# Earlier loads, fewer low-rank passes and split sums in a hybrid encoder block

## The chip, the cores and the metric

The kernel runs on one core of one Trainium2 chip. The metric is the device time of one launch in microseconds (us), as the median of repeated runs; beside it there is one profiled execution with a trace. The engines are PE (TensorE, matrix products), DVE (VectorE), ACT (ScalarE), POOL (GpSimd, hardly used here) and SP (SyncE, which issues all DMAs of this kernel).

## The reference

One layer of an encoder block on x of 1024 tokens by 1024 features in float32: a gated linear attention (GLA) branch and a windowed attention branch from one input projection, then a SwiGLU feed-forward.

```python
h = _rms_norm(x, norm_mix_g[l])
proj = h @ w_in[l]
(g_q, g_k, g_v, g_r, g_lr_f, g_lr_b,
 s_q, s_k, s_v, gate_a, gate_b) = jnp.split(proj, split_at, axis=-1)
y_gla = _gla_branch(...) @ w_o_gla[l]      # log gate: log_sigmoid(lr @ up + bias) / 16, lr has rank 16 each way
y_swa = _swa_branch(...) @ w_o_swa[l]      # banded attention in blocks of 128, 8 heads on 2 key heads
merged = jax.nn.sigmoid(gate_a) * y_gla + jax.nn.sigmoid(gate_b) * y_swa
x = x + merged @ w_out[l]
h2 = _rms_norm(x, norm_ffn_g[l])
gu = h2 @ w_ffn_in[l]
x = x + (jax.nn.silu(gu[..., :D_FF]) * gu[..., D_FF:]) @ w_ffn_out[l]   # D_FF = 2816
```

The low-rank codes `g_lr_f` and `g_lr_b` are 16 columns each, 32 in all.

## The kernel before

Everything is kept transposed: features on the 128 partitions, tokens along the free dimension in two halves of 512 (`s` = 0, 1). A product in float32 is made of three matmuls in fp32r (`mm3`): each operand is split into a high part (an fp32r copy made on ACT) and a low part (the rest, subtracted on DVE), and high x high, high x low and low x high are summed in PSUM. `wunit` loads a weight unit (`wr`) and splits it so (`wh`, `wl`). Most big products run in a scheme with fewer block products and more additions (lines L300 to L302 for the first stage).

The order of PE's instructions is written out by hand (`tc.manual_schedule` for PE); the other engines' orders are set by a scheduler that knows the dependences. All tiles come from pools; a tag with one buffer is used again only when its last user has finished, and a pool that is opened later can lie on the memory of one that has been closed, with waits on that memory's last users.

The places that the change touches, in order of time:

- **The low-rank codes** (`lr_mm`). The weights are 32 columns repeated three times, 96 wide, in two units of four k-tiles. For each of 8 k-tiles and 2 halves there are three matmuls into a 96-row PSUM tile. The 96 rows go to DRAM (`keep_raw`), and later come back as `lrf`, are multiplied with the norm's factor `rstd` and split into `lrS` (high, low and high again in its three groups of 32 rows), beside the gate's up-projection (`upr`, split to `upS`). The gate matmul is `ch<-lrS,upS`. `upr` and `lrf` live in the pool `ip`.
- **Sums over partitions.** A matmul of ones with the summed squares (`acc`) adds over the partitions and broadcasts the sum; `rsqrt` makes `rstd` of it (Ln and Exp on ACT, then a Newton step of four instructions on DVE, L101 to L104). In the first stage it is called for both halves one after the other, with the buffers "rsl" and "rst" of pool `w0`; `out_stats` does the same late in the kernel.
- **Attention** runs in slots (`todo`); each slot's stages are laid between dense matmuls of another projection (`fill`). `k_prep` and `a_prep` load a block of keys and values (`kvr`, one buffer) or of queries (`qr`, two) from DRAM and normalise it at once. `st` (L186) is the copy of dense results out of PSUM on ACT.
- **The second feed-forward product** (`fo_product`) follows the last call of `ffn_in`. For each step `k` it loads and splits an input (`hload`: `hr`, `hh`, `hl`) and a weight (`a`, split to `wh`, `wl`) and issues 12 matmuls (L1169).

Of the kernel before, what the change touches and what calls it, by code (L numbers as in the profile page):

```python
# [8 lines left out]
F32 = mybir.dt.float32  # L9
# [5 lines left out]
P = 128  # L15
# [15 lines left out]
def body(tc, i, out):  # L31
    nc = tc.nc
    with ExitStack() as root:
# [49 lines left out]
        nc.scalar.preload_act_table_set("natural_log_exp_and_others")  # L83

        g1 = load_const(cst, "g1", i["g1"], (P, KT))
        ones = cst.tile([P, P], F32, tag="ones", name="ones")
        nc.vector.memset(ones, 1.0)
        epst = cst.tile([P, 1], F32, tag="eps", name="eps")
        nc.vector.memset(epst, EPS)
        eps128 = cst.tile([P, 1], F32, tag="eps128", name="eps128")  # L90
# [123 lines left out]
                done = t  # L214


        def lr_mm(b, u):
            h, l = wunit(i["w_lr"][u], 384)
            for kk in range(4):
                k = u * 4 + kk  # L220
                c = slice(kk * 96, (kk + 1) * 96)
                for s in range(2):
                    mm3(b[s][:96], h[:, c], l[:, c], xh[k][s], xl[k][s], k == 0, k == KT - 1)

# [148 lines left out]
        with tc.manual_schedule(engines={mybir.EngineType.PE}):  # L373
            xr[0, 0] = x_load(0, 0)

            wu = chtile((P, 512))
            for _ in range(12):
                mm(wu[:, :P], ones, ones, True, True)
            bq = [[mmtile(), mmtile()] for _ in range(2)]
            us = [wunit(i["w_f"][m, 0]) for m in range(2)]  # L380
            xr[0, 1] = x_load(0, 1)
            for k in range(KT):
                if k < KT - 1:
                    for s in range(2):
# [12 lines left out]
            for u in range(2):  # L397
                lr_mm(bl, u)
            for m in range(2):
                for s in range(2):  # L400
                    keep_raw(("q0", "k0")[m], s, bq[m][s])
            for s in range(2):
                keep_raw("lr", s, bl[s], 96)
            for k in range(KT):
                for s in range(2):
                    x_square(k, s)
            for f in range(0, NG, 2):
                x_first(f)
                if f == 0:
                    for s in range(2):  # L410
                        v = chtile((P, HT))
                        mm(v, ones, acc[s], True, True)
                        rsqrt(rstd[:, s * HT:(s + 1) * HT], v, 1.0 / T, EPS, epst, w0, (P, HT), "", ("rsl", "rst"))
                    vt = chtile((P, KT, 2))
                    for t in range(KT):
                        mm(vt[:, t], acc[t // 4][:, (t % 4) * P:(t % 4 + 1) * P], ones[:, 0:2], True, True)
                    rsqrt(rstdt, vt[:, :, 0], 1.0 / T, EPS, epst, pad, (P, KT), "rt")
                for k in range(2):
                    xcombos(f % 4 + k, f // 4)
            for f in range(NG):  # L420
                x_two(f)
                if f == NG - 1:
                    for k in range(4):
                        r = x_load(k, 1, True)
                        xh[k][1] = xp.tile([P, HT], FR, tag=f"xh{k}1", name=nm("xh"))
                        xl[k][1] = xp.tile([P, HT], FR, tag=f"xl{k}1", name=nm("xl"))
                        x_split(xh[k][1], xl[k][1], r, g1[:, k:k + 1])
                if f:
                    x_last(f - 1)
                x_four(f)  # L430
            x_last(NG - 1)
# [18 lines left out]
        lrf = ip.tile([96, T], F32, tag="lrf", name="lrf")  # L450
        for s in range(2):
            c = slice(s * HT, (s + 1) * HT)
            nc.sync.dma_start(out=lrf[:, c], in_=scr["lr", s][:96])
            nc.vector.tensor_tensor(lrf[:, c], lrf[:, c], rstd[:96, c], op=ALU.mult)
        nc.scalar.activation(lrS[0:96], lrf, AF.Copy)
        nc.vector.tensor_tensor(lrS[32:64], lrf[32:64], lrS[32:64].bitcast(F32), op=ALU.subtract)
# [266 lines left out]

        keys, att = {}, {}

        def k_prep(t):
            kv = sw.tile([P, 4, P], F32, tag="kvr", name=nm("kvr"), bufs=1)
            need(("skv", t))
            nc.sync.dma_start(out=kv.rearrange("p a b -> p (a b)"), in_=scr["skv", t])
            v2 = kv[:, 2:4].rearrange("p a b -> p (a b)")  # L730
            nc.scalar.activation(vSh[t], v2, AF.Copy)
            nc.vector.tensor_tensor(vSl[t], v2, vSh[t].bitcast(F32), op=ALU.subtract)
            keys[t] = norm_rope(kv[:, 0:2], 2, t, kg, 1.0 / 128, EPS, epst)
# [8 lines left out]

        def a_prep(g, n):
            a = att[g, n] = Chunk()
            need((f"sq{g}", n))
            qr = sw.tile([P, 4, P], F32, tag="qr", name=nm("qr"))
            nc.sync.dma_start(out=qr.rearrange("p a b -> p (a b)"), in_=scr[f"sq{g}", n])
# [105 lines left out]
        for n in range(2 * KT):  # L853
# [9 lines left out]
        order = (a_probs, k_prep, a_prep, a_scores, a_turn, k_turn, a_out)  # L863
# [213 lines left out]
        def ffn_in(f, between):  # L1077
# [27 lines left out]
            product(X, wsplit(F.r22, 512), YX["T4"], 4, False, True)  # L1105
            c21, g0 = ctile("c21"), F.g0
            nc.vector.tensor_tensor(c21, X, p1, op=ALU.add)
            nc.vector.tensor_tensor(c21, c21, g0, op=ALU.mult)
            nc.vector.tensor_tensor(c22, c22, u2, op=ALU.mult)
            put("B1" if f < DK else "B2", 1, f % DK, c21)  # L1110
            put("B1" if f < DK else "B2", 2, f % DK, c22)

            if f < DK:
                t1 = hp.tile([P, HT], F32, tag="tx", name=nm("tx"), bufs=4)
# [18 lines left out]
        later = []  # L1133
        steps = [0]

        def hload(key, k, th, tl):
            r = fo1.tile([P, HT], F32, tag="hr", name=nm("hr"), bufs=6)
# [18 lines left out]
        def fo_product(ys, q, key, start, stop, before, after, th=None, tl=None):  # L1156
            for k in range(DK):
                before(k)
                if not (th and tl):
                    steps[0] += 1  # L1160
                pool = fo3 if steps[0] % 3 == 2 else hp
                x = hload(key, k, (th[0], f"a{th[1]}{k}") if th else (pool, "hh"),
                          (tl[0], f"a{tl[1]}{k}") if tl else (pool, "hl"))
                w = wsplit(aq[q, k], 512)
# [27 lines left out]
        with tc.manual_schedule(engines={mybir.EngineType.PE}):  # L1192
# [12 lines left out]
            for k in range(4):  # L1205
# [78 lines left out]
def _layout(n):  # L1284
# [12 lines left out]
    lr = np.tile(w[:, 3072:3104], (1, 3)).reshape(2, 4, P, 96)  # L1297
    d["w_lr"] = np.ascontiguousarray(lr.transpose(0, 2, 1, 3)).reshape(2, P, 384)
# [53 lines left out]
```

## Time and profile before

| | us |
|---|---|
| median of 3 runs | 1671.59 (1671.16 to 1672.97) |
| profiled execution | 1674.78 |
| its span, first to last instruction | 1673.0 |
| PE busy | 1655.1 |
| DVE busy | 1260.0 |
| ACT busy | 892.7 |

The mean granted TensorE clock was 0.998. In a row of the timeline the first number is the start in us, the second the time of the instruction (or of all of a group, with its count as x4), and the bracket at the end tells how long the engine had been idle and what released it. Matmuls overlap, so the time from one start to the next is what one costs. In a row of the waits stand the total, the count and the longest. A row with two times and a colon is a stretch of the span: its length, the busy time of each engine with its count of instructions, the granted clock, the DMA share and GB/s.

### The profile page before, as it was taken

The numbers are of one execution on the slowest core, as the hardware profiler recorded it, in microseconds if no ns is written. First come the engines' busy times: TensorE is split into PE (matmuls) and PEld (weight loads), VectorE is DVE, ScalarE is ACT, GpSimd is POOL, SyncE is SP. The second block draws the span as 40 slices with busy tenths as digits, with TensorE's granted clock in tenths as the row PEclk, the third lists the DMA queues.
The fourth block names the chain that finished last, engine by engine and source line by source line (L and its number), as shares of the span: only waits on it lengthen the run. The fifth ranks groups of instructions, "written<-read, shape, count | busy, mean of one in ns | idle before, by whom it ended". The sixth has DMA issues, their size and how long they took to land.

```text
span 1673.0 us, 23709 instructions
## 1 busy us (share of the span) xinstructions
PE 1655.1 (99%) x7808; PEld 1373.8 (82%) x7808; DVE 1260.0 (75%) x2615; ACT 892.7 (53%) x1881; POOL 0.2 (0%) x4
## 2 busy tenths in 40 slices
PE   9999999999999999999999999999999999999999
PEld 7888888888888788877888888888888888788887
DVE  8756767888874799856886679887778778779755
ACT  8522465687877488776554556433333333354443
POOL 0000000000000000000000000000000000000000
PEclk9999999999999999999999999999999999999999
DMA  7444453344434643227866645353234443496533
GB/s 234 139 137 152 142 158 94 108 139 125 134 114 153 190 133 102 89 76 242 261 215 188 174 141 170 108 170 101 89 110 154 152 145 126 164 333 195 149 97 120
DMA packets 157067, 251.88 MB, mean 151 GB/s; under 512 B 17966, under 2 KB 43438, under 8 KB 156944
## 3 DMA queue, kind: packets, MB, share of 16 engines
q1 hardware_dynamic: 156944, 250.37, 47.9%
q8 instruction: 61, 1.00, 0.3%
q14 instruction: 62, 0.51, 0.1%
HBM read 182.80 MB, written 67.50 MB: 150 GB/s over the span
## 4 chain that ended last, share of the span: by engine, by line
PE 87%; ACT 5%; DVE 4%; DMA 3%; issue 1%; SPq 0%; ACTq 0%; DVEq 0%
PE mm L76 33%; PE mm L300 8%; PE mm L302 7%; PE mm L301 7%; PE ch L76 7%; PE mm L1169 7%; PE ch L1169 5%; PE ch L302 3%; PE ch L300 3%; PE ch L301 3%; PE ch L813 1%; DMA kvr<-skv 1%; ACT p L796 1%; DMA lo<-b 1%; ACT p L802 0%
## 5 line engine op out<-in xcount | busy, mean ns | idle before, releaser
L70 ACT ACTIVATE wh<-wr 128x512 fp32r<-128x512 f32 (+1 forms) x240 | 149.6, 628 | 101.2 <-PE mm L76 75.9
L72 DVE TENSOR_TENSOR wl<-wr,wh 128x512 fp32r<-128x512 f32 (+1 forms) x240 | 164.0, 686 | 45.8 <-ACT wh L70 45.2
L292 ACT ACTIVATE wh<-ws 128x512 fp32r<-128x512 f32 x120 | 76.0, 634 | 178.5 <-PE mm L301 89.1
L76 PE MATMUL mm<-wh,xh 128*128 128x512 f32 x320 | 127.0, 397 | 3.5 <-ACT st L186 3.5
L76 PE MATMUL mm<-wl,xh 128*128 128x512 f32 x320 | 128.2, 401 | 0.0
L76 PE MATMUL mm<-wh,xl 128*128 128x512 f32 x320 | 127.1, 397 | 0.0
L76 PE MATMUL mm<-xh,wh 128*128 128x512 f32 x256 | 103.4, 404 | 0.8 <-ACT wh L70 0.6
L76 PE MATMUL mm<-xl,wh 128*128 128x512 f32 x256 | 101.2, 395 | 0.3 <-DVE xl L245 0.3
L293 DVE TENSOR_TENSOR wl<-ws,wh 128x512 fp32r<-128x512 f32 x120 | 82.4, 687 | 21.6 <-ACT wh L292 21.6
L292 ACT ACTIVATE wh<-wr 128x512 fp32r<-128x512 f32 x60 | 38.0, 634 | 105.3 <-issue 49.5
L292 ACT ACTIVATE wh<-a 128x512 fp32r<-128x512 f32 x66 | 41.9, 635 | 90.3 <-PE ch L1169 42.2
L76 PE MATMUL mm<-xh,wl 128*128 128x512 f32 x256 | 87.7, 405 | 0.0
L293 DVE TENSOR_TENSOR wl<-a,wh 128x512 fp32r<-128x512 f32 x66 | 45.6, 691 | 41.7 <-ACT wh L292 41.3
L76 PEld LDWEIGHTS mm<-wh,xh 128*128 128x128 f32 x320 | 60.6, 189 | 14.4 <-ACT st L186 3.9
L1169 PE MATMUL mm<-hh,wh 128*128 128x512 f32 x176 | 69.1, 392 | 1.4 <-ACT hh L1141 1.4
L1169 PE MATMUL mm<-hl,wh 128*128 128x512 f32 x176 | 69.3, 394 | 0.7 <-DVE hl L1142 0.7
L1169 PE MATMUL mm<-hh,wl 128*128 128x512 f32 x176 | 69.2, 393 | 0.0
L76 PEld LDWEIGHTS mm<-wh,xl 128*128 128x128 f32 x320 | 60.6, 189 | 10.5
L76 PEld LDWEIGHTS mm<-wl,xh 128*128 128x128 f32 x320 | 60.6, 189 | 10.1
L1142 DVE TENSOR_TENSOR hl<-hr,hh 128x512 fp32r<-128x512 f32 x77 | 52.9, 687 | 6.5 <-ACT hh L1141 6.4
L76 PEld LDWEIGHTS mm<-xh,wh 128*128 128x128 f32 x256 | 48.2, 188 | 7.4 <-ACT wh L70 0.8
L76 PEld LDWEIGHTS mm<-xl,wh 128*128 128x128 f32 x256 | 48.2, 188 | 7.3 <-DVE xl L245 0.8
(574 smaller groups left out, 4892.3 us busy)
## 6 DMA issues: line engine op xcount, KB each, us to landing
wr<-in_w_fi_dram SPq DMA_DIRECT2D x102, 256.0 KB, 2.8
wr<-in_w_f_dram SPq DMA_DIRECT2D x80, 256.0 KB, 2.9
wr<-in_w_t_dram SPq DMA_DIRECT2D x80, 256.0 KB, 2.8
B<-c SPq DMA_DIRECT2D x44, 256.0 KB, 2.1
T<-tx SPq DMA_DIRECT2D x44, 256.0 KB, 2.6
a<-in_w_fo_dram SPq DMA_DIRECT2D x44, 256.0 KB, 5.3
hr<-T SPq DMA_DIRECT2D x44, 256.0 KB, 2.7
hr<-B SPq DMA_DIRECT2D x33, 256.0 KB, 4.2
```

The costliest lines, as they stand in the source:

```text
L70: nc.scalar.activation(h, raw, AF.Copy)
L72: nc.vector.tensor_tensor(l, raw, h.bitcast(F32), op=ALU.subtract)
L76: nc.tensor.matmul(o, a, b, start=start, stop=stop)
L292: nc.scalar.activation(h, src, AF.Copy)
L293: nc.vector.tensor_tensor(l, src, h.bitcast(F32), op=ALU.subtract)
L300: nc.tensor.matmul(o, h[:, c], x[kk][0], start=start and kk == 0, stop=False, skip_group_check=True)
L301: nc.tensor.matmul(o, h[:, c], x[kk][1], start=False, stop=False, skip_group_check=True)
L302: nc.tensor.matmul(o, l[:, c], x[kk][0], start=False, stop=kk == nk - 1, skip_group_check=True)
L796: nc.scalar.activation(p[:, h, :w], p[:, h, :w], AF.Exp, bias=nm_[:, h:h + 1], scale=a.rs[:, h:h + 1], accum_out=dn[:, h:h + 1])
L813: nc.tensor.transpose(pt[:, h], a.p[:, h, (kb - a.b0) * P:(kb - a.b0 + 1) * P], ident)
L1142: nc.vector.tensor_tensor(l, r, h.bitcast(F32), op=ALU.subtract)
L1169: nc.tensor.matmul(ys[m], a[:, c], b, start=f0, stop=f1, skip_group_check=True)
```

## The change

Five edits.

1. Low-rank codes: the weight is loaded as 32 columns per k-tile and its high and low part stand side by side in one 64-column operand. Per k-tile and half there is one matmul of the 64 columns with the high part of x and one of the 32 high columns with its low part. The 64 rows in DRAM hold two partial sums, which are added after loading, in three groups of 32 rows, through a new tile `lrb` in `ip` (one buffer).
2. `part_sum`: the sum over partitions takes a split `acc`, two fp32r matmuls in place of one in f32. The parts use the tags of `rsqrt`'s buffers.
3. Attention: the loads are stages of their own (`k_load`, `a_load`), one slot ahead of `k_prep` and `a_prep`, at the end of the slot's stages.
4. The first two steps of the second feed-forward product are loaded at the start of the last `ffn_in`, and their weights split ahead of its last product.
5. In the last `ffn_in` the two gated products (`c21`, `c22`) are put off to later steps.

```diff
-        ones = cst.tile([P, P], F32, tag="ones", name="ones")
+        onesr = cst.tile([P, P], FR, tag="ones", name="ones")
+        ones = onesr.bitcast(F32)
+        def part_sum(v, a, pool):
+            h = pool.tile([P, HT], FR, tag="rsl", name=nm("ah"))
+            l = pool.tile([P, HT], FR, tag="rst", name=nm("al"))
+            nc.scalar.activation(h, a, AF.Copy)
+            nc.vector.tensor_tensor(l, a, h.bitcast(F32), op=ALU.subtract)
+            mm(v, onesr, h, True, False)
+            mm(v, onesr, l, False, True)
...
-                    mm3(b[s][:96], h[:, c], l[:, c], xh[k][s], xl[k][s], k == 0, k == KT - 1)
+                    nc.tensor.matmul(b[s][:64], w[:, k].rearrange("p a b -> p (a b)"), xh[k][s], start=k == 0,
+                                     stop=False, skip_group_check=True)
+                    nc.tensor.matmul(b[s][:32], w[:, k, 0], xl[k][s], start=False, stop=k == KT - 1,
+                                     skip_group_check=True)
...
-                        mm(v, ones, acc[s], True, True)
+                        part_sum(v, acc[s], w0)
...
-            nc.sync.dma_start(out=lrf[:, c], in_=scr["lr", s][:96])
+            lrb = ip.tile([96, HT], F32, tag="lrb", name=nm("lrb"))
+            for g in range(3):
+                nc.sync.dma_start(out=lrf[32 * g:32 * g + 32, c], in_=scr["lr", s][0:32])
+                nc.sync.dma_start(out=lrb[32 * g:32 * g + 32], in_=scr["lr", s][32:64])
+            nc.vector.tensor_tensor(lrf[:, c], lrf[:, c], lrb, op=ALU.add)
...
+        def k_load(t):
+            raws[t] = sw.tile([P, 4, P], F32, tag="kvr", name=nm("kvr"), bufs=1)
+            need(("skv", t))
+            nc.sync.dma_start(out=raws[t].rearrange("p a b -> p (a b)"), in_=scr["skv", t])
+        def a_load(g, n):
+            need((f"sq{g}", n))
+            raws[g, n] = sw.tile([P, 4, P], F32, tag="qr", name=nm("qr"))
+            nc.sync.dma_start(out=raws[g, n].rearrange("p a b -> p (a b)"), in_=scr[f"sq{g}", n])
...
+                if n:
+                    todo[n - 1].append((k_load, n))
+            todo[n].append((a_load, g, t))
+        order = (a_probs, k_prep, a_prep, a_scores, a_turn, k_turn, a_out, k_load, a_load)
+        k_load(0)
...
-            mm(v, ones, acc[:, s * HT:(s + 1) * HT], True, True)
+            part_sum(v, acc[:, s * HT:(s + 1) * HT], fi)
...
+            w = wsplit(F.r22, 512)
+            if f == NFF - 1:
+                for k in range(2):
+                    r, x = early[k]
+                    early[k] = (x, wsplit(r, 512))
+            product(X, w, YX["T4"], 4, False, True)
...
+                    later.append(lambda v=v: gated(*v))
...
+                if th and tl and k < len(early):
+                    x, w = early[k]
...
+                if f == NFF - 1:
+                    for k in range(2):
+                        r = ctile("oc")
+                        nc.sync.dma_start(out=r, in_=i["w_fo"][k, 0])
+                        early.append([r, hload(("B1", 1), k, (hp, "hh"), (hp, "hl"), ctile("oc"))])
```

How the engines' orders change at the places that matter. The names are tiles (output, then inputs), and the brackets the semaphores that the instruction waits for. First PE at the two sums of the first stage, before:

```order
L302 MATMUL mm_478<-xh_101,wl_545 128x512
L76 MATMUL ch_563<-acc_136,ones 128x512
L76 MATMUL ch_573<-acc_137,ones 128x512 [waits PE_49]
L76 MATMUL ch_583<-ones,acc_136 128x2 x4
L76 MATMUL ch_583<-ones,acc_137 128x2 x4
L300 MATMUL mm_622<-xh_87,wh_626 128x512
```

And now:

```order
L76 MATMUL ch_540<-ah_541,ones 128x512
L76 MATMUL ch_540<-al_542,ones 128x512 [waits DVE_49]
L76 MATMUL ch_555<-ah_556,ones 128x512 [waits PE_49,Activation_49]
L76 MATMUL ch_555<-al_557,ones 128x512 [waits DVE_49]
L76 MATMUL ch_570<-ones,acc_136 128x2 [waits PE_49]
```

DVE there, now, from the first step of the first half's rsqrt (`rt_550`) to the subtraction of the second half (`al_557`); the other rows are the combinations of x that later products need:

```order
L111 TENSOR_SCALAR rt_550<-ch_540 128x512 [waits Activation_49]
L278 TENSOR_TENSOR T4l_820<-xr_253,T4h_819 128x512 [waits Activation_49]
L112 TENSOR_TENSOR rt_550<-rt_550,rl_547 128x512 [waits DVE_49,Activation_49]
L278 TENSOR_TENSOR T3l_911<-xr_193,T3h_910 128x512 [waits Activation_49]
L113 SCALAR_TENSOR_TENSOR rt_550<-rt_550,rl_547 128x512 [waits DVE_49]
L297 SCALAR_TENSOR_TENSOR xr_285<-xr_285,g_70,xr_287 128x512
L114 SCALAR_TENSOR_TENSOR rstd<-rt_550,rl_547 128x512 [waits DVE_49]
L295 SCALAR_TENSOR_TENSOR xr_213<-xr_213,ng_134,xr_307 128x512
L278 TENSOR_TENSOR T4l_916<-xr_285,T4h_915 128x512 [waits Activation_49]
L94 TENSOR_TENSOR al_557<-acc_137,ah_556 128x512 [waits Activation_49]
```

The subtraction for the second sum now stands behind the last step of the first half's rsqrt; there was no such instruction before. Next, SP at the end of the first stage, before. `gb` and `ga` are its last stores, `upr` and `lrf` the gate's loads, `wr` weights:

```order
L63 DMA tri<-in_c_tri_dram 128x128 [waits DMAHW4_49,DVE_49]
L445 DMA upr<-in_up_dram 98x1024 [waits DMAHW5_49]
L453 DMA lrf<-lr_427 96x512 [waits DMAHW6_49]
L453 DMA lrf<-lr_431 96x512 [waits DMAHW7_49]
L68 DMA wr_2024<-in_w_t_dram 128x512 [waits DMAHW0_49,DVE_49]
L306 DMA gb_0_1813<-xc_368_1811 128x512 [waits DMAHW1_49,DVE_49]
L68 DMA wr_2042<-in_w_t_dram 128x512 [waits DMAHW2_49,DVE_49]
L306 DMA gb_1_1835<-xc_372_1833 128x512 [waits DMAHW3_49,DVE_49]
L68 DMA wr_2060<-in_w_t_dram 128x512 [waits DMAHW4_49,DVE_49]
L306 DMA ga_1_1856<-xu_353_1769 128x512 [waits DMAHW5_49,DVE_49]
L68 DMA wr_2078<-in_w_t_dram 128x512 [waits DMAHW6_49,DVE_49]
L306 DMA gb_0_1876<-xc_378_1874 128x512 [waits DMAHW7_49,DVE_49]
```

And now:

```order
L322 DMA ga_1_1843<-xu_353_1756 128x512 [waits DMAHW1_49,DVE_49]
L68 DMA wr_2079<-in_w_t_dram 128x512 [waits DMAHW2_49,DVE_49]
L322 DMA gb_0_1863<-xc_378_1861 128x512 [waits DMAHW3_49,DVE_49]
L68 DMA wr_2097<-in_w_t_dram 128x512 [waits DMAHW4_49,DVE_49]
L460 DMA upr<-in_up_dram 98x1024 [waits DMAHW5_49,DMAHW7_49,DMAHW3_49,DMAHW1_49]
L470 DMA lrf<-lr_404 32x512 [waits DMAHW6_49]
L471 DMA lrb_1891<-lr_404 32x512
L470 DMA lrf<-lr_404 32x512 [waits DMAHW0_49]
```

The load of `upr` has moved behind the last store of the stage and waits for four transfers in place of one. Last, ACT in attention's start, before:

```order
L99 ACTIVATE rl_7019<-rl_7019 128x4 [waits Activation_49]
L186 ACTIVATE st_6941<-mm_6697,rstdt 128x512 [waits PE_49]
L186 ACTIVATE st_6977<-mm_6698,rstdt 128x512 [waits PE_49]
L186 ACTIVATE st_6987<-mm_6699,rstdt 128x512 [waits PE_49]
L70 ACTIVATE wh_7044<-wr_7042 128x512 [waits DMAHW3_49,PE_49]
L98 ACTIVATE rl_7132<-ss_7128,eps_76 128x4 [waits DVE_49]
L731 ACTIVATE vSh_6785<-kvr_6946 128x256 [waits DMAHW1_49]
L695 ACTIVATE sq_6950<-kvr_6946 128x256
L186 ACTIVATE st_6997<-mm_6700,rstdt 128x512 [waits PE_49]
```

And now:

```order
L196 ACTIVATE st_6946<-mm_6698,rstdt 128x512 [waits PE_49]
L196 ACTIVATE st_6980<-mm_6699,rstdt 128x512 [waits PE_49]
L196 ACTIVATE st_6990<-mm_6700,rstdt 128x512 [waits PE_49]
L714 ACTIVATE sq_7220<-qr_7182 128x512 [waits DMAHW0_49,DVE_49]
L70 ACTIVATE wh_7050<-wr_7048 128x512 [waits DMAHW4_49,PE_49]
L196 ACTIVATE st_7018<-mm_6701,rstdt 128x512 [waits PE_49]
L760 ACTIVATE vSh_6786<-kvr_6881 128x256 [waits DMAHW2_49]
```

The fourth `st` has moved ahead of `vSh`, and a step on the third block of queries (`sq<-qr`) has moved ahead of that `st`.

More of the change, by code (lines that the diff above doesn't have):

```diff
@@ L214, in slot, with lr_mm @@
                 done = t
[L217 to L221, printed above, removed]
+        def lr_mm(b):
+            raw = wp.tile([P, KT, 32], F32, tag="wr", name=nm("wr"), bufs=4)
+            nc.sync.dma_start(out=raw, in_=i["w_lr"])
+            w = wp.tile([P, KT, 2, 32], FR, tag="wh", name=nm("wh"), bufs=5)
+            nc.scalar.activation(w[:, :, 0], raw, AF.Copy)
+            nc.vector.tensor_tensor(w[:, :, 1], raw, w[:, :, 0].bitcast(F32), op=ALU.subtract)
+            for k in range(KT):
                 for s in range(2):
-                    mm3(b[s][:96], h[:, c], l[:, c], xh[k][s], xl[k][s], k == 0, k == KT - 1)
+                    nc.tensor.matmul(b[s][:64], w[:, k].rearrange("p a b -> p (a b)"), xh[k][s], start=k == 0,
+                                     stop=False, skip_group_check=True)
+                    nc.tensor.matmul(b[s][:32], w[:, k, 0], xl[k][s], start=False, stop=k == KT - 1,
+                                     skip_group_check=True)
         g0s = ExitStack()
@@ L396, in body @@
             bl = [chtile((P, 512)), chtile((P, 512))]
-            for u in range(2):
-                lr_mm(bl, u)
+            lr_mm(bl)
             for m in range(2):
@@ L402, in body @@
             for s in range(2):
-                keep_raw("lr", s, bl[s], 96)
+                keep_raw("lr", s, bl[s], 64)
             for k in range(KT):
@@ L724, in body @@
         keys, att = {}, {}
+        raws = {}
+        def k_load(t):
[6 more added lines that the diff above has]
+            nc.sync.dma_start(out=raws[g, n].rearrange("p a b -> p (a b)"), in_=scr[f"sq{g}", n])
         def k_prep(t):
-            kv = sw.tile([P, 4, P], F32, tag="kvr", name=nm("kvr"), bufs=1)
-            need(("skv", t))
-            nc.sync.dma_start(out=kv.rearrange("p a b -> p (a b)"), in_=scr["skv", t])
+            kv = raws.pop(t)
             v2 = kv[:, 2:4].rearrange("p a b -> p (a b)")
@@ L744, in a_prep @@
             a = att[g, n] = Chunk()
-            need((f"sq{g}", n))
-            qr = sw.tile([P, 4, P], F32, tag="qr", name=nm("qr"))
-            nc.sync.dma_start(out=qr.rearrange("p a b -> p (a b)"), in_=scr[f"sq{g}", n])
+            qr = raws.pop((g, n))
             b = sw.tile([P, 4, P], F32, tag="sq4", name=nm("sq"))
@@ L1104, in ffn_in, with gated @@
             nc.vector.tensor_tensor(u2, u2, r1, op=ALU.mult)
-            product(X, wsplit(F.r22, 512), YX["T4"], 4, False, True)
+            w = wsplit(F.r22, 512)
[4 more added lines that the diff above has]
+            product(X, w, YX["T4"], 4, False, True)
             c21, g0 = ctile("c21"), F.g0
             nc.vector.tensor_tensor(c21, X, p1, op=ALU.add)
[L1108 to L1111, printed above, removed]
+            def gated(j, c, g):
+                nc.vector.tensor_tensor(c, c, g, op=ALU.mult)
+                put("B1" if f < DK else "B2", j, f % DK, c)
+            for v in ((1, c21, g0), (2, c22, u2)):
+                if f < NFF - 1:
+                    gated(*v)
+                else:
+                    later.append(lambda v=v: gated(*v))
             if f < DK:
@@ L1134, in body, with hload @@
         steps = [0]
-        def hload(key, k, th, tl):
-            r = fo1.tile([P, HT], F32, tag="hr", name=nm("hr"), bufs=6)
+        early = []
+        def hload(key, k, th, tl, r=None):
+            if r is None:
+                r = fo1.tile([P, HT], F32, tag="hr", name=nm("hr"), bufs=6)
             nc.sync.dma_start(out=r, in_=scr[(*key, k)])
@@ L1296, in _layout @@
     d["w_t"] = np.ascontiguousarray(np.stack([a.reshape(KT, P, 512) for a in wt]))
-    lr = np.tile(w[:, 3072:3104], (1, 3)).reshape(2, 4, P, 96)
-    d["w_lr"] = np.ascontiguousarray(lr.transpose(0, 2, 1, 3)).reshape(2, P, 384)
+    d["w_lr"] = np.ascontiguousarray(w[:, 3072:3104].reshape(KT, P, 32).transpose(1, 0, 2))
     up = np.zeros((98, 2, 512), f)
```

8 lines of the change are left out of this document (4 added, 4 removed).

## The prediction

> **What bounds the kernel now.** I read the busy shares first, then the chain that ended last.
>
> ```profile
> PE 1655.1 (99%) x7808; PEld 1373.8 (82%) x7808; DVE 1260.0 (75%) x2615; ACT 892.7 (53%) x1881; POOL 0.2 (0%) x4
> PE 87%; ACT 5%; DVE 4%; DMA 3%; issue 1%; SPq 0%; ACTq 0%; DVEq 0%
> ```
>
> PE (TensorE) is busy 1655.1 of 1673.0 us, so it is idle for 18 us in all. Two things shorten such a kernel: fewer PE slots, and the removal of a wait of PE. Any new wait of PE is paid in full, because PE has no slack later in which to make it good. The waits of PE, largest first:
>
> ```profile
> PE mm L76 <- ACT st L186: 3.5, 1, 3.5
> PE mm L1169 <- ACT hh L1141: 1.4, 1, 1.4
> PE mm L1169 <- DVE hl L1142: 0.7, 1, 0.7
> ```
>
> The first is in attention; the other two are the start of the second feed-forward product. Both are places that the change touches.
>
> **Low-rank codes.** 48 matmuls become 32 of the same 512 columns.
>
> ```profile
> 29.46 11.09 PE ch L76 x48
> 197.88 5.44 PE mm L76 x24
> 203.32 0.24 PE ch L76 x2
> ```
>
> On the chain one of the 48 takes 11.09 / 48 = 0.231 us with 96 weight columns, and one of 24 dense ones 5.44 / 24 = 0.227 us with 128. The width of the weights does not set the time, so 64 and 32 columns cost the same slot: 16 fewer are **-3.7 us**, as PE works back to back there.
>
> **Sums over partitions.** Each f32 matmul becomes two on split operands.
>
> ```profile
> 51.28 1.88 PE L76 MATMUL ch<-acc,ones 128*128 128x512 f32 x4
> 52.99 1.84 PE L76 MATMUL ch<-ones,acc 128*128 128x2 f32 x16
> ```
>
> Two sums (four records) take 52.99 - 51.28 = 1.71 us, 0.855 each; two split matmuls take 0.454. Four sums save **-1.6 us**. The two late sums (the output's statistics) have their own free buffers and their accumulators are done us ahead, so I take their copy and subtraction as hidden: 0 to +1 us if they are not.
>
> The second sum of the first stage is another matter. Its high and low parts use the buffers "rsl" and "rst", one each, and the first sum's rsqrt uses the same two until its last step. So the second sum, which follows the first at once on PE, has to wait for the whole rsqrt of the first: Ln, Exp, four steps on DVE, then its own copy and subtraction.
>
> ```profile
> 32.66 0.69 DVE L253 TENSOR_TENSOR acc<-acc,sq 128x512 f32<-128x512 f32 x1 [0.19 <-ACT sq L251]
> 53.34 0.71 DVE L72 TENSOR_TENSOR wl<-wr,wh 128x512 fp32r<-128x512 f32 x1
> 57.17 0.69 DVE L104 SCALAR_TENSOR_TENSOR rstd<-rt,rl 128x512 f32<-128x512 f32 x1
> 53.08 0.68 ACT L98 ACTIVATE rl<-ch,eps 128x512 f32<-128x512 f32 x1
> 54.17 0.62 ACT L99 ACTIVATE rl<-rl 128x512 f32<-128x512 f32 x1
> ```
>
> DVE is a full queue from 32.66 on: 40 places later, two of them tiny, it runs the last step of the first rsqrt at 57.17: (24.5 - 0.3) / 38 = 0.64 us each. In the changed order that step stands 34 places behind the same add: 32.66 + 34 x 0.64 = 54.4, ending at 55.1, less some 0.5 us because one split of the low-rank weights fewer stands ahead: 54.6. The copy on ACT takes some 0.6, like the Exp, and by the place of the subtraction, third behind the last step, DVE ends it near 56.4. PE reaches this point at 51.28 - 3.70 = 47.6, does the first sum until 48.0, and could do both matmuls of the second at once; the last of them cannot start before 56.4. Idle: 56.4 - 48.0 - 0.2 = **+8.2 us**. Bounds: 5.4 if DVE's queue were empty (0.68 + 0.62 + 4 x 0.69 + 0.62 + 0.69), 10 if Ln and Exp get stuck behind neighbours on ACT.
>
> **The gate's loads.** Smaller codes mean more loads and two added sums, but what decides is where the load of the gate's up-projection (upr) stands. Its pool has grown by a tile of 2 KB per partition (lrb) and now reaches into memory whose last users are the final stores of the first stage. In the order of SP the load stood ahead of those stores; now it stands behind the last one and waits for it to land.
>
> ```profile
> 187.08 4.54 DMA upr<-in_up_dram
> 199.21 0.32 SPq L306 DMA_DIRECT2D gb<-xc  x1
> 202.60 0.32 SPq L483 DMA_DIRECT2D qk<-q  x1
> 191.72 1.06 ACT L446 ACTIVATE upS<-upr 98x1024 fp32r<-98x1024 f32 x1 [1.91 <-DMA upr<-in_up_dram]
> 192.15 0.69 DVE L454 TENSOR_TENSOR lrf<-lrf,rstd 96x512 f32<-96x512 f32 x1 [1.16 <-DMA lrf<-lr]
> 192.87 1.22 DVE L447 TENSOR_TENSOR upS<-upr,upS 34x1024 fp32r<-34x1024 f32 x1
> 195.44 1.07 ACT L455 ACTIVATE lrS<-lrf 96x1024 fp32r<-96x1024 f32 x1 [0.26 <-DVE lrf L454]
> 196.64 1.22 DVE L456 TENSOR_TENSOR lrS<-lrf,lrS 32x1024 fp32r<-32x1024 f32 x1
> qk<-q SPq DMA_DIRECT2D x2, 128.0 KB, 2.4
> ```
>
> Before, the codes were ready at 196.64 + 1.22 = 197.9 and the first gate matmul ran at 203.32: 5.4 us to spare. The load of qk waited for the same last store and was issued at 202.60, so upr is issued about then (a time of before; where PE is earlier or later all of this moves along). Then, in series: upr 4.54, copy 1.06, subtraction 1.22, add 0.69, the second half's lrb (one buffer, three issues and a landing like qk's, 0.9 + 2.4), add and multiply 1.38, copy 1.07, subtraction 1.22: 14.5 us, to 217.1. PE gets there at 203.32, so 13.8; the last store can go out some 0.5 us sooner because DVE no longer does the gate's work ahead of it: **+13.3 us**. Bounds: 10.5 if the loads of both halves overlap and land in 2 us, 15 if the twelve small loads queue. PE's order is fixed by hand, so nothing steps in front of the gate matmul; later dense weights are ready by the time it runs.
>
> **Attention.** One wait goes:
>
> ```profile
> 560.50 4.88 DMA kvr<-skv
> 565.41 0.42 ACT L731 ACTIVATE vSh<-kvr 128x256 fp32r<-128x256 f32 x1 [2.04 <-DMA kvr<-skv]
> 566.04 0.67 ACT L186 ACTIVATE st<-mm,rstdt 128x512 f32<-128x512 f32 x1
> 566.76 0.50 PE L76 MATMUL mm<-wh,xh 128*128 128x512 f32 x1 [3.45 <-ACT st L186]
> 567.45 0.63 PE L76 MATMUL mm<-wh,xl 128*128 128x512 f32 x1
> 570.01 0.63 PE L76 MATMUL mm<-wh,xl 128*128 128x512 f32 x1
> 566.80:570.40 3.60, 3.60 (x9) 2.85 (x10) 3.43 (x13) 1.95 (x6) 0.00 (x0) 0.55 0.66 215
> ```
>
> ACT stood at vSh for a load, and the copy out of PSUM (st) that PE needed was behind it. The load still goes to a single buffer and was issued the moment that it was free, so it will hardly land sooner; what helps is that this st now stands ahead of vSh on ACT. A third query load now stands ahead of the st, which I put at 0.7 us of wait left. Then there is the price after the wait: six matmuls from 567.45 to 570.01 are 0.427 us apart instead of 0.227, at a granted clock of 0.55, so about 1.4 us are lost after the wait itself. Gain 3.5 + 1.5 - 0.7 = **-4.3 us** (0 to -5). In the other slots the transposes come some 15 matmuls sooner on PE, 3.4 us; I allow half of that either way.
>
> **Second feed-forward.** Its first two steps' inputs and weights are loaded and split during the last feature.
>
> ```profile
> 1452.65 0.33 SPq L1150 DMA_DIRECT2D a<-in_w_fo_dram  x1
> 1450.00:1455.00 5.00, 5.00 (x24) 4.10 (x22) 2.24 (x4) 0.63 (x1) 0.00 (x0) 1.00 0.27 69
> 1454.95 0.39 PE L302 MATMUL mm<-bt43h,wl 128*128 128x512 f32 x1
> 1456.70 0.49 PE L1169 MATMUL mm<-hh,wh 128*128 128x512 f32 x1 [1.36 <-ACT hh L1141]
> 1457.93 0.72 PE L1169 MATMUL mm<-hl,wh 128*128 128x512 f32 x1 [0.73 <-DVE hl L1142]
> 1459.13 0.63 PE L1169 MATMUL mm<-hh,wh 128*128 128x512 f32 x1
> 1460.83 0.63 PE L1169 MATMUL mm<-hl,wh 128*128 128x512 f32 x1
> 1457.90:1461.20 3.30, 3.27 (x7) 2.36 (x8) 2.81 (x5) 1.95 (x4) 0.00 (x0) 0.52 0.98 356
> ```
>
> From 1454.95 to 1459.13 five slots should take 1.1 us and take 4.2; then some five more are 0.425 apart, at a granted clock of 0.52. That is 3.1 + 1.2 = **-4.3 us**. Two steps are 24 matmuls, 5.4 us of cover, and the third step's load is issued when the first one's was, about 1452.65; by the same steps of loading and splitting it is ready some 1 us ahead of need. Two extra weight loads of 256 KB fall where the DMA share is 0.27. Kept: 0 to -4.4.
>
> **The clock after a wait.** Both long waits above are followed by some 3.5 us at 0.52 to 0.55. The two new ones, 8.2 and 13.3 us, are longer, so I charge each 1.4 us: **+2.8**. The Trainium skill, "TensorE: Matmul & The Clock Gate", section "What's actually happening", says that after an idle window of about 3.4 us the array runs at half clock until it has been busy for about as long; this trace agrees (0.55 over 3.6 us after 3.45 us of idling). By the page each wait would cost 1.7 us, an estimate from it, and the sum would be 0.6 us higher. It speaks against this change.
>
> **Sum.** -3.7 - 1.6 - 4.3 - 4.3 = -13.9; +8.2 + 13.3 + 2.8 = +24.3; together **+10.4 us**. The profiled execution took 1674.8 us (span 1673.0), so 1685.2 by its clock; the median shown is 1671.59, 3.2 lower, and I forecast against that: **1682.0 us**. Within 0.2% (3.3 us) I call it the same.
>
> **The rivals.**
> A. The sum as it stands, 1676 to 1688 by the bounds above: 60%.
> B. The gate matmul is not late: the stores land well before 202.60 (that row shows only when the next load was issued), or the loads that follow are quick. Price 14.7, so -4.3 and 1667.3. It ends on the other side when the loss there, clock included, is below 1.0 us. For it speaks the 5.4 us to spare before; against it, upr and the two splits behind it alone take 6.8 us after the last store was issued at 199.21. 9%.
> C. The second sum does not wait long, because its buffers come free while PE is still behind. Price 9.6: +0.8, 1672.4. Against it speaks the 5.4 us of the shortest chain. 9%.
> D. Neither wait shows: -13.9, 1657.7. 11%.
> E. The new waits come and attention keeps its own, since its load lands no sooner and another evacuation is caught behind it: +14.7, 1686.3, more if the twelve small loads queue. 11%.
>
> A and E are slower; B and D faster; C about the same, with the edges of B and C: slower 0.73, same 0.09, faster 0.18. The range runs from 1666, which leaves out D, to 1689.
>
> **What the profile would show.** The codes: 32 matmuls in 7.4 us. The second sum: PE idle for some 8 us near 48 us with ACT's ah or DVE's al as releaser, then half clock. The gate: upr issued after the last gb store and PE idle for some 13 us before the first matmul of lrS, released by DVE. Attention: no wait near 566 over 1 us. Second feed-forward: 0.23 us from step to step at the start. I am wrong if either of the new waits is missing, or if PE finds a wait there that begins later and ends sooner than the chains above say; the weakest number is the gate's, eight steps in series of which two are small loads never timed in this trace.

## The result

The changed kernel takes 1688.58 us in the median of 5 runs (1686.35 to 1690.55) against 1671.59 us (1670.74 to 1674.23): slower, ratio 1.0099 with a 95% interval of 1.0085 to 1.0114. The forecast was 1682.0. The profiled execution took 1690.42 us with a span of 1688.6, 15.6 more than before.

Busy time and chain of the changed kernel:

```profile
PE 1655.4 (98%) x7792; PEld 1373.5 (81%) x7792; DVE 1263.7 (75%) x2620; ACT 892.0 (53%) x1884; POOL 0.2 (0%) x4
PE 87%; DVE 5%; ACT 3%; DMA 3%; issue 1%; SPq 0%; DVEq 0%; ACTq 0%
```

There are sixteen matmuls fewer, and PE is busy as long as before: some matmuls must have run slower. The span has grown by idle time. The waits of PE (total, count, longest):

```profile
PE ch L76 <- DVE lrS L475: 12.2, 1, 12.2
PE ch L76 <- ACT ah L93: 6.9, 1, 6.9
PE ch L76 <- DVE pl L844: 1.5, 1, 1.5
...
PE ch L76 <- DVE kTl L770: 0.9, 1, 0.9
...
PE mm L76 <- ACT obh L868: 0.6, 1, 0.6
```

The two large waits of before (st at 566, hh and hl at 1456) are gone from the head of the list. Two larger ones stand there: the gate matmul and the second sum.

The second sum in PE's timeline, and the clock behind it (stretch, length, busy times, granted clock, DMA share, GB/s):

```profile
47.13 0.40 PE L76 MATMUL ch<-al,ones 128*128 128x512 f32 x1
54.39 0.80 PE L76 MATMUL ch<-ah,ones 128*128 128x512 f32 x1 [6.87 <-ACT ah L93]
55.54 0.80 PE L76 MATMUL ch<-al,ones 128*128 128x512 f32 x1 [0.35 <-DVE al L94]
56.13 3.41 PE L76 MATMUL ch<-ones,acc 128*128 128x2 f32 x16
54.40:58.00 3.60, 3.25 (x12) 2.65 (x12) 3.04 (x5) 1.23 (x2) 0.00 (x0) 0.50 0.02 5
62.00:63.50 1.50, 1.50 (x5) 1.11 (x5) 1.17 (x4) 0.00 (x0) 0.00 (x0) 0.50 0.00 0
64.00:66.00 2.00, 2.00 (x10) 1.60 (x10) 0.69 (x1) 1.11 (x2) 0.00 (x0) 1.00 0.00 0
```

The second sum's last matmul ran at 55.54, where 56.4 was forecast. But the clock stayed at one half until about 63.8, 9.4 us after the restart, and the sixteen small matmuls (the rows `128x2`) took 3.41 us where they had taken 1.84.

The gate: three rows of SP's timeline, then pieces of the chain that ended last (start, time, what):

```profile
205.05 0.33 SPq L322 DMA_DIRECT2D gb<-xc  x1
207.58 0.40 SPq L460 DMA_DIRECT2D upr<-in_up_dram  x1
215.23 1.24 SPq L471 DMA_DIRECT2D lrb<-lr  x3
205.05 2.46 DMA gb<-xc
212.18 1.06 ACT upS L461
214.52 0.70 DVE lrf L472
216.05 1.92 DMA lrb<-lr
218.14 0.70 DVE lrf L472
218.86 0.70 DVE lrf L473
219.59 1.06 ACT lrS L474
220.67 1.23 DVE lrS L475
221.94 0.79 PE ch L76 x2
```

Here upr is issued 2.5 us after the last store gb, when that has landed, and the gate matmul follows 221.94 - 207.58 = 14.4 us later; the forecast's chain had 14.5.

The start of the second feed-forward product:

```profile
1474.07 0.39 PE L1217 MATMUL mm<-hh,wh 128*128 128x512 f32 x1
1475.89 0.39 PE L1217 MATMUL mm<-hh,wl 128*128 128x512 f32 x1
```

Eight steps in 1.82 us, 0.227 each, with no wait.

Taking the start of the same matmul in both traces gives an account of where the time went:

| stretch (us of before) | measured | forecast |
|---|---|---|
| to 40.4: low-rank codes (0.7 of it in the first 9 us) | -4.4 | -3.7 |
| both sums of the first stage, to 53.0 | +7.5 | +8.2 - 0.8 |
| half clock behind them, to 56.9 | +3.4 | +1.4 |
| wait before the gate matmul, at 203.2 | +12.2 | +13.3 |
| half clock behind it, to 206.4 | +2.8 | +1.4 |
| attention, to 775.8 | -1.5 | -4.3 |
| late sums, to 1063 | -1.2 | -0.8 |
| start of the second feed-forward, to 1460.8 | -4.0 | -4.3 |
| its sixth step, to the end | +0.8 | 0 |
| all (from figures before rounding) | +15.7 | +10.4 |

### The profile page after: what moved, and what is told of

It reads as the page before. It is cut to its first block, busy times and chain, and to the rows that moved or that the text cites. A ratio compares the mean times of both kernels' runs of the same rounds, so it can differ in the third digit from the quotient of the medians.

```text
span 1688.6 us, 23701 instructions
## 1 busy us (share of the span) xinstructions
PE 1655.4 (98%) x7792; PEld 1373.5 (81%) x7792; DVE 1263.7 (75%) x2620; ACT 892.0 (53%) x1884; POOL 0.2 (0%) x4
## 4 chain that ended last, share of the span: by engine, by line
PE 87%; DVE 5%; ACT 3%; DMA 3%; issue 1%; SPq 0%; DVEq 0%; ACTq 0%
PE mm L76 32%; PE mm L316 8%; PE mm L317 8%; PE mm L318 8%; PE mm L1217 7%; PE ch L76 7%; PE ch L1217 5%; PE ch L317 3%; PE ch L318 3%; PE ch L316 3%; PE ch L840 1%; DVE wl L72 0%; DMA gb<-gb 0%; PE ch L647 0%; DMA kvr<-skv 0%
## 5 line engine op out<-in xcount | busy, mean ns | idle before, releaser
L70 ACT ACTIVATE wh<-wr 128x512 fp32r<-128x512 f32 x238 | 148.4, 628 | 111.7 <-PE mm L76 80.2
L72 DVE TENSOR_TENSOR wl<-wr,wh 128x512 fp32r<-128x512 f32 x238 | 162.5, 686 | 54.8 <-ACT wh L70 52.0
L308 ACT ACTIVATE wh<-wr 128x512 fp32r<-128x512 f32 x60 | 37.9, 632 | 104.0 <-issue 48.1
```

The source lines that it names most:

```text
L70: nc.scalar.activation(h, raw, AF.Copy)
L72: nc.vector.tensor_tensor(l, raw, h.bitcast(F32), op=ALU.subtract)
L308: nc.scalar.activation(h, src, AF.Copy)
```

## The experiments

**The gate's loads.** The first run puts the second parts of the codes into lrS, which is free at that time:

```diff
-            lrb = ip.tile([96, HT], F32, tag="lrb", name=nm("lrb"))
+            lrb = lrS[0:96, c].bitcast(F32)
```

> The changed kernel, with the second parts of the low-rank codes loaded into lrS (which is overwritten only later) in place of the new tile lrb, so that the pool ip keeps its old size; the twelve loads and the two additions stay. Theory (the pool's reach moves upr behind the last store): upr is issued near 186 us again, the wait of 12.2 us before the first gate matmul goes and with it 2.8 us of half clock behind it: 15 us faster than the changed kernel, about 1673.5. Rival (the small loads and additions are late in themselves): upr early, but 5 to 10 us of wait remain, 1679 to 1684.

Measured: 1682.54 us, 6.0 faster than the changed kernel; the rival's range. The waits of PE, then rows of SP and DVE of this run:

```profile
PE ch L76 <- DVE lrS L475: 3.9, 1, 3.9
PE mm L76 <- DVE xc L386: 1.9, 1, 1.9
194.30 0.46 SPq L460 DMA_DIRECT2D upr<-in_up_dram  x1
205.29 0.58 SPq L471 DMA_DIRECT2D lrS<-lr  x1
208.75 0.34 SPq L322 DMA_DIRECT2D gb<-xc  x1
209.62 0.42 SPq L471 DMA_DIRECT2D lrS<-lr  x1
206.71 0.69 DVE L472 TENSOR_TENSOR lrf<-lrf,lrS 96x512 f32<-96x512 f32 x1 [3.15 <-DMA lrS<-lr]
208.04 0.68 DVE L386 TENSOR_TENSOR xc<-mm,xp 128x512 f32<-128x512 f32 x1
```

The pool's reach is half of the story: upr is issued ahead of the last four stores again and its 14 us chain is gone. But now the twelve loads alternate with the stores in SP's order. The first addition holds DVE for 3.15 us, xc behind it is late, PE waits for xc, its store gb is late too, and the last loads stand behind that store.

The next run takes the additions and most of the loads away from there: DVE adds the two parts straight from PSUM before they are stored.

```diff
-                keep_raw("lr", s, bl[s], 64)
+                c = ep.tile([P, HT], F32, tag="c", name=nm("c"), bufs=2)
+                nc.scalar.copy(c[:32], bl[s][:32])
+                nc.vector.tensor_tensor(c[:32], c[:32], bl[s][32:64], op=ALU.add)
+                scr["lr", s] = scratch(f"lr_{s}")
+                for g in range(3):
+                    nc.sync.dma_start(out=scr["lr", s][32 * g:32 * g + 32], in_=c[:32])
...
+            nc.sync.dma_start(out=lrf[:, c], in_=scr["lr", s][:96])
```

> The changed kernel, with the two parts of the low-rank codes added on DVE before they are stored (32 rows, stored three times), so that the later stage is that of before: two loads, no additions, no lrb, upr ahead of the last stores. The 32 matmuls stay. Theory: no wait at the gate matmul and none for xc beside it, 15 us faster than the changed kernel, about 1673.5. Rival (the first gate matmul is late because PE arrives 4 us sooner): 2 to 5 us of wait remain, 1676 to 1679.

Measured: 1674.69 us, 13.9 faster than the changed kernel and below the rival's range. No wait for lrS or xc of half a microsecond is left. So the saved matmuls cost nothing later if the codes reach the gate as they did before.

**The second sum.**

```diff
-                        part_sum(v, acc[s], w0)
+                        part_sum(v, acc[s], w0) if s == 0 else mm(v, ones, acc[s], True, True)
```

> The changed kernel, with the second of the first stage's two sums as one f32 matmul again (the first stays split), so that nothing of it needs the buffers of rsqrt. Theory: the wait near 48 us goes (7.3 us) and the half clock behind it (3.4 us), the sum costs 0.4 us more: 10.3 us faster than the changed kernel, about 1678.3. Rival (the half clock there comes from the sixteen matmuls of two columns behind the sums, which do little work): the wait goes, the half clock stays, 1681.7.

Measured: 1676.78 us, 11.8 faster than the changed kernel, 1.5 more than the theory had. The wait and all of the half clock behind it are gone with it, sixteen small matmuls or not.

The next run asks why the clock came back so late there.

```diff
                 if f == 0:
+                    vt = chtile((P, KT, 2))
+                    for t in range(KT):
+                        mm(vt[:, t], acc[t // 4][:, (t % 4) * P:(t % 4 + 1) * P], ones[:, 0:2], True, True)
                     for s in range(2):
                         v = chtile((P, HT))
                         part_sum(v, acc[s], w0)
...
-                    vt = chtile((P, KT, 2))
-                    for t in range(KT):
-                        mm(vt[:, t], acc[t // 4][:, (t % 4) * P:(t % 4 + 1) * P], ones[:, 0:2], True, True)
```

> The changed kernel, with the sixteen matmuls of two columns put ahead of the two split sums on PE in place of behind them; nothing else. After the wait dense matmuls then follow at once. Theory (the sixteen, which hardly use the array, put off the return of the full clock, which took 9.4 us there and 5.7 us after the gate's longer wait): full clock 4 to 6 us after the second sum; the sixteen now lie under the wait; some 3 us faster than the changed kernel, 1685.5. Rival (the slow time depends on the wait alone or on chance): slow for 8 to 10 us again, about 4 us of it lost in dense matmuls, 1687 to 1688.

Measured: 1684.92 us (1683.84 to 1685.85), 3.7 faster than the changed kernel and below the rival's range. The wait is 5.6 us, and behind it:

```profile
55.50:58.50 3.00, 3.00 (x7) 2.08 (x8) 3.00 (x6) 2.07 (x4) 0.00 (x0) 0.50 0.00 0
59.00:61.00 2.00, 2.00 (x10) 1.63 (x9) 1.96 (x4) 0.77 (x3) 0.00 (x0) 1.00 0.00 0
```

The slow time is 3.45 us (55.35 to 58.80) in place of 9.4. It is one profile each, but the direction is that of the theory: dense matmuls behind the wait bring the clock back, the sixteen matmuls of two columns did not. Only a part of the 6 us between the two is theirs; the last section divides it.

The third way keeps both sums split and writes them ahead of the first rsqrt. It starts from the kernel with the codes added early; the "mended kernel" that it is compared with has the second sum in f32 as well and is measured further down:

```diff
+                    vs = []
                     for s in range(2):
                         v = chtile((P, HT))
+                        vs.append(v)
                         part_sum(v, acc[s], w0)
+                    for s in range(2):
+                        v = vs[s]
                         rsqrt(...)
```

> The mended kernel with both sums of the first stage split, but both written ahead of the first rsqrt, so that the second's parts wait for the two matmuls of the first sum and not for its rsqrt. Theory: the wait is one copy on ACT and one subtraction on DVE with DVE's queue before it, 1.5 to 3 us; no slow clock, since it is shorter than the waits that had one: 1664 to 1666, 1.5 to 3 us slower than the mended kernel. Rival (any split of the second sum waits as long): 1672 or more.

Measured: 1665.08 us, inside the theory's range. The waits are short, as thought, but "no slow clock" was wrong:

```profile
PE ch L76 <- ACT ah L93: 1.0, 1, 1.0
PE ch L76 <- DVE al L94: 0.8, 1, 0.8
50.20:57.30 7.10, 7.10 (x28) 6.13 (x27) 3.77 (x9) 1.26 (x4) 0.00 (x0) 0.56 0.07 26
```

Two waits of 1.0 and 0.8 us, with one matmul between them and the sixteen small ones behind, were followed by 7 us at 0.56.

**Attention.** The edit alone (`k_load`, `a_load` and the order of stages), on the kernel before:

> The kernel before with the attention edit alone. Theory (the loads as stages of their own take a share of the dense matmuls, so the stages that compute have fewer between them and wait more): the wait near 566 goes, 5 us with its half clock, but 3 to 3.5 us come back in small waits from 570 to 800: 1.5 us faster than before, 1670.1. Rival (the prediction's term): 4.3 us faster, 1667.3.

Measured: 1671.95 us, ratio 1.0000 (0.9991 to 1.0008). The wait near 566 is gone, and the time comes back elsewhere; the interval excludes the prediction's 4.3 us, and the theory's 1.5 lie at its edge. Two runs split the edit. In one the loads come a slot ahead but PE's order is that of before:

```diff
+                ahead = [e for e in v if e[0] in (k_load, a_load)]
+                v = [e for e in v if e[0] not in (k_load, a_load)]
                 slot([lambda e=e: e[0](*e[1:]) for e in v], ...)
+                for e in ahead:
+                    e[0](*e[1:])
```

> The kernel before with attention's loads a slot ahead, but put behind the slot's dense matmuls in place of being stages of their own: PE's order is then that of before, row for row, and on ACT the copy st stands behind vSh as before. Theory (what took the wait near 566 us away was the other spread of the dense matmuls over the slot, which moved st ahead of vSh, not the earlier loads): the wait stays at 2 to 3.5 us, 1672 to 1672.5. Rival (the loads ahead are the gain, the spread the loss): the wait goes and nothing comes back, 4 to 5 us faster, 1667.5.

Measured: 1672.76 us, ratio 1.0002 (0.9993 to 1.0011). The wait stays:

```profile
PE mm L76 <- ACT st L186: 2.6, 1, 2.6
```

In the other the loads are where they were, and empty stages alone spread the dense matmuls:

```diff
+                if n:
+                    todo[n - 1].append((k_none, n))
+            todo[n].append((a_none, g, t))
```

> The kernel before with its loads where they were, and with one empty stage in a slot for each load that the change moves, so that the dense matmuls are spread as in the changed kernel (PE's order is then that of the attention edit alone, row for row). Theory: as the attention edit alone, the wait near 566 us gone and the same small waits at 580 to 640 and 770 to 780, 1671.5 to 1672.5. Rival (loads): the wait near 566 stays and small waits are added, 2 to 3 us slower than before, 1674.5 to 1675.5.

Measured: 1673.16 us, ratio 1.0006 (0.9997 to 1.0014), 0.7 us above the theory's range and below the rival's. The wait at st is gone, and in its place stand two others, which the attention edit alone has too (1.5 us each there):

```profile
PE ch L76 <- DVE kTl L741: 2.1, 1, 2.1
PE ch L76 <- DVE pl L817: 1.5, 1, 1.5
```

So the earlier loads do nothing that shows here (the interval of their run reaches from -1.2 to +1.8 us). What took the wait away is the other spread, which puts st ahead of vSh on ACT; and the same spread leaves fewer dense matmuls between the stages that compute, so that their chains through ACT and DVE show.

**The second feed-forward alone**: the change's edits in `ffn_in`, `hload` and `fo_product`, on the kernel before.

> The kernel before with the edit of the second feed-forward alone (first two steps loaded ahead, gated products put off). Theory (from the two traces side by side): 4.0 us come at the start, 0.8 us go again as a wait at the sixth step, 3.2 us faster, 1668.4. Rival (the prediction's term): 4.3 us faster and no new wait, 1667.3.

Measured: 1667.64 us, ratio 0.9969 (0.9960 to 0.9979), 5 us faster: the 3.2 us of the theory were too few, and the rival's 4.3 are nearer. At the start of the product the trace shows 4.5 us gained, and later one wait of 0.2 us; the wait at st also happened to be 2.2 us in this execution, which is not the edit's. The waits of 0.4 and 0.3 us at the sixth step of the changed kernel's trace came again in the run with the loads into lrS (0.6 and 0.2), but in no other run with this edit, so they are not put down to the edit by itself; their cause stays open.

**The mends together.** The codes added early and the second sum in f32, both diffs as above:

> The changed kernel with both mends: the codes added before they are stored (as in the run just before) and the second of the first stage's sums in f32 (as two runs of the last group before). Theory (the waits are separate and add): 15 us less than the second sum's run, 1661.8, some 10.5 us faster than before. Rival (with one wait gone the next comes to light, since everything arrives 15 us sooner): 1665 to 1669.

Measured: 1662.81 us, ratio 0.9947 (0.9933 to 0.9960). The mends add: 25.8 us together, 11.8 and 13.9 alone. Without the attention edit:

> The mended kernel with the attention edit taken out. Theory (the edit is worth nothing in sum): 1662 to 1664. Rival (it is worth the 4.3 us of the prediction once the other waits are gone): 1667.

Measured: 1663.84 us, ratio 0.9953 (0.9939 to 0.9967), inside the theory's range; the runs with and without the edit overlap (1661.61 to 1664.67 and 1662.97 to 1666.40). And with the spread in the first two slots alone, where it moves st, and nowhere else:

```diff
+                if n and n - 1 < 2:
+                    todo[n - 1].append((k_none, n))
+            if n < 2:
+                todo[n].append((a_none, g, t))
```

> The mended kernel without the attention edit, but with empty stages in attention's first two slots alone, which move st ahead of vSh as the edit did and leave PE's order of the later slots as it was before. Theory: the wait near 566 us goes as in the changed kernel, and the small waits from 580 to 640 are not there: 4 us faster than the next kernel of this group and some 3 us faster than the mended kernel, 1659 to 1660. Rival (the later waits came from the loss of time in the first slots, not from the spread of the later ones): as the mended kernel, 1662.8.

Measured: 1660.84 us (1660.37 to 1661.89), ratio 0.9932 (0.9919 to 0.9944); the best of all, 3.0 us below the run without the attention edit, where some 4 were expected, and 0.8 above the theory's range. Its largest waits of PE:

```profile
PE ch L76 <- DVE sh L577: 1.1, 3, 0.7
PE ch L76 <- DVE eps L101: 1.0, 1, 1.0
```

## Why the prediction was right, and where not

The direction and its reasons held. Both new waits are where they were forecast, released by the instructions that were named, and within 1.1 us of their size. The median moved by 17.0 us where 10.4 was forecast, so it came out 0.4 us inside the upper end of the range, and 0.6 us above that of the forecast's own case A (1676 to 1688). That it is inside is partly luck: the five runs lie on both sides of 1689, and what some terms lacked is partly made up for by others that were too large. Case E, with 1686.3 the nearest price, is not what happened: attention's wait at st did go. The steps:

- **Low-rank codes**: -3.7, as measured between 29 and 40 us. The row of 0.231 per matmul was enough.
- **Second sum**: +8.2 less 0.8 against +7.5. The agreement is closer than its parts: PE waited 7.2 us, 1.0 less than forecast, but the four matmuls, two of them at half clock, took 2.0 us in place of the 0.9 forecast. The run with an f32 second sum confirms the cause.
- **Gate**: +13.3 against +12.2. The chain from upr to the gate matmul was right within 0.1 us; upr was issued 1 us sooner, set against PE, than forecast. The forecast took over the 3.4 us from the issue of the last store to that of qk, which waited for it before; in the changed kernel that store landed after 2.46 us (the row `DMA gb<-xc` of the chain). Why it was quicker stays open. The pool's reach is shown as the cause of upr's place. The old place of upr alone is not enough: the run with the loads into lrS has it and is still 7.9 us slower than the run with the codes added early (1682.54 against 1674.69). The forecast had the queueing of the twelve small loads only as a bound of the gate's term.
- **Clock after a wait**: the term that failed most. 1.4 us each were taken from the one slow stretch whose start and end were quoted; 3.4 and 2.8 were lost. The length of a slow stretch is no constant: 3.7 us at 566 before, 5.7 behind the gate, 9.4 behind the sums. The last section shows what sets it.
- **Attention**: the other term that failed. -4.3 was forecast and -1.5 came in this trace, about nothing in the timed runs of the edit alone. The gain at st was real. The allowance of +-1.7 for the other slots was the right place and too small, and was taken as nothing in the sum.
- **Second feed-forward**: -4.3 against -4.0 in this trace and -4.5 alone (in the forecast's working, five steps of 0.2 us are 1.0 and not 1.2). The 0.8 us at the sixth step were not forecast.
- **Late sums**: hidden, as said.

The terms that were too small add up to 3.4 for the clock, 2.8 for attention and 1.1 for the second feed-forward, 7.3 less 2.0 from the others: the 5.3 us between +10.4 and +15.7. Another 1.3 us lie between the profiled executions and the medians, within the spread of the runs.

## What to carry to other kernels

Where one engine has no slack, ask of each new small tile which freed memory its pool now covers, and of each reused buffer whose last step releases it; the orders of the engines gave both new waits here to about a microsecond. Price a new wait of PE with its slow clock, as a range and not from one stretch, and look at what follows the wait: small matmuls there made it longer. And when a step that is moved also changes how filler work is spread, test the two apart.

## What the runs showed of the hardware

After a wait PE ran at a granted clock of 0.50 for 3.45 to 5.7 us when dense matmuls followed (55.35 to 58.80 with the small ones moved; behind the gate) and for 9.4 us when sixteen matmuls of two columns came first. The length of the wait alone does not decide: in the mended kernel without the attention edit, PE waited 3.5 us and went on at full clock:

```profile
PE mm L76 <- ACT st L196: 3.5, 1, 3.5
561.80:565.00 3.20, 3.20 (x15) 2.63 (x16) 3.04 (x13) 1.81 (x7) 0.00 (x0) 1.00 0.63 216
```

while 1.0 and 0.8 us with little work between and behind were followed by 7 us at 0.56. What the traces have in common is a fixed step. Here are whole stretches at half clock, with the part of them that lies in the wait: one of the kernel before, two of the changed kernel, one with the small sums first and one with both sums split ahead of the first rsqrt.

```profile
567.17:570.58 3.41, 3.41 (x10) 2.67 (x9) 3.32 (x12) 1.58 (x6) 0.00 (x0) 0.50 0.69 225
50.20:63.86 13.66, 9.12 (x29) 7.55 (x30) 10.18 (x20) 3.95 (x8) 0.00 (x0) 0.50 0.04 16
214.04:227.70 13.66, 5.76 (x15) 4.60 (x16) 8.33 (x17) 4.27 (x6) 0.00 (x0) 0.50 0.33 90
51.96:58.78 6.82, 3.43 (x7) 2.44 (x8) 6.80 (x15) 3.47 (x7) 0.00 (x0) 0.50 0.00 1
51.02:57.84 6.82, 6.82 (x21) 5.76 (x22) 2.97 (x7) 0.96 (x4) 0.00 (x0) 0.50 0.01 2
```

They last 1, 4, 4, 2 and 2 times 3.41 us, and in the changed kernel the second begins 48 such steps after the first (214.04 - 50.20 = 163.84). Cut each trace into cells of that length, so that the edges fall on these times. In all of the traces kept, apart from their first and last microseconds, the clock halved behind a cell with little work for PE and came back behind the first cell that dense matmuls filled (3.0 us or more of 3.41). The cells below show what was little. Two with 1.57 and 1.74 us of work, across which the wait of 3.5 us above is spread, kept the full clock (the edges of that trace are counted from 7.08, where its first dense matmuls come to full speed: 0.77 us at 6.18, 0.40 at 7.14); the fullest cell of dense matmuls that halved it held 1.34 us (attention edit alone, 1452.05 to 1455.47). The third, with both sums split, has 1.67 us of work, half of it small matmuls, and the clock halved behind it. The last two are from the run with the codes added early: the first of them holds 0.5 us of a dense matmul and then small matmuls alone, and the clock stayed at one half through the next.

```profile
556.63:560.04 3.41, 1.57 (x7) 0.95 (x6) 2.70 (x9) 0.30 (x1) 0.00 (x0) 1.00 0.83 180
560.04:563.45 3.41, 1.74 (x8) 1.43 (x9) 2.47 (x11) 3.08 (x9) 0.00 (x0) 1.00 0.88 335
47.60:51.02 3.42, 1.67 (x11) 1.32 (x11) 3.40 (x6) 2.70 (x5) 0.00 (x0) 1.00 0.65 219
55.40:58.81 3.41, 3.41 (x16) 3.31 (x16) 2.41 (x4) 0.69 (x1) 0.00 (x0) 0.50 0.02 5
58.81:62.22 3.41, 3.41 (x10) 2.83 (x11) 2.19 (x6) 1.92 (x5) 0.00 (x0) 0.50 0.00 0
```

So the small matmuls counted here as little work, however busy PE looked. This divides the 9.4 us of the changed kernel. PE restarted there at 54.39, in the cell from 53.62 to 57.03; with dense matmuls at once the next cell would have been full and the clock back at 60.44, 6.05 us after the restart (an estimate from the cells). The small ones cost one cell more, 3.4 us. The 3.45 us with the small sums first are the least possible by these cells, and luck: PE restarted at 55.35, and a cell began at 55.37. By the same estimate a wait that empties a cell costs half of one to two cells, 1.7 to 3.4 us, when dense matmuls follow at once; the forecast's 1.4 lay below that.

The Trainium skill, "TensorE: Matmul & The Clock Gate", section "What's actually happening", describes a window of about 3.4 us that runs freely and in which the activity of the array is watched. These traces agree, with steps of 3.41 us.
